# A token loop of the first mixture-of-experts layer, moved from ahead of the last down product to between the sixth and the seventh expert tile

## The chip, the cores and the metric

One core of one Trainium2 chip. The metric is the time of one execution of the whole kernel in device microseconds. The kernel before has a median of 1263.22 us.

## The reference

Two layers over 256 tokens and 256 context tokens of width 1024. Each layer has a mixer (differential attention, latent attention and retention side by side), a layer norm, a grouped mixture of 16 experts with two experts to a token, and a second layer norm. The first layer (l = 0) routes all 512 rows through its experts, the second only the 256 tokens. The change is inside the first layer's mixture:

```python
def moe(tokens, router_w, router_b, w1, w3, w2):
    scores = jax.nn.sigmoid((tokens @ router_w).astype(jnp.float32))
    choice = scores + router_b.astype(jnp.float32)
    ...
    gates = jnp.sum(jax.nn.one_hot(eidx, N_EXPERTS, ...) * wsel[..., None], 1)

    def expert_step(acc, p):
        w1e, w3e, w2e, ge = p
        y = (jax.nn.silu(tokens @ w1e) * (tokens @ w3e)) @ w2e
        return acc + ge[:, None] * y, None
    out, _ = lax.scan(expert_step, jnp.zeros_like(tokens), (w1, w3, w2, gates.T))
    return out
```

w1 and w3 are 1024 x 512 and w2 is 512 x 1024 for each expert, all in 32-bit floats.

## The kernel before, in words

**Expert tiles.** The mixture of the first layer is cut into twelve tiles of 128 token places (`PLANS[0]`, NX = 12). A tile of one expert has all its places for that expert; a tile of two shares them between two. In order of work the tiles are: one, one, two, one, one, two, one, two, one, two, one, one. Step t of the loop over tiles writes `up(t)` (the products with w1 and w3, L1625 for one expert, L1653 for two), then `tokens(t + 1)` (the next tile's rows are turned, L2003), then `down(t - 1)` (the product with w2, L1625 or L1750). `hidden` (L1668) turns the gated hidden rows; `combine` (L2033, L2036) brings a tile's result back to token order; `ones_at` and `transposed_ones` (L1617) make the 0/1 matrices for that; `lists` make the next index list (L1601) and gather rows by it (L1982). TensorE's order is the order in which this is written (`manual_schedule(engines=only_pe)`); the other engines' order is planned by the scheduler.

**Weights.** For a tile of one expert each weight piece of 128 x 2048 (1 MB) is split in two halves of 128 x 1024: `wsplit` casts the high part on ACT (`wh`), and DVE (640 columns) and POOL (384 columns, L1231) make the low part (`wl`); then three products are made from high and low parts. A tile of two experts uses its weights as they came. A `Stream` loads the pieces in order into a ring of ten buffers: SP issues a load (L184 as two halves of 512 KB, L188 as one of 1 MB) as soon as a buffer comes free, so that the order of loads is fixed and buffers set their pace. Up to eight of SP's loads are under way at a time.

**Rows by token.** Down products of tiles 0 to 6 (`BY_ROWS` = 7) are written as rows to a buffer in memory: ACT issues `yd<-rows` (L1688), two of 256 KB for a tile. `token_rows` (L1972) gathers them for each token at step t = 9, on POOL, in eight gathers.

**The loop.** A tile has a fixed number of places. For tokens that found none there is a loop, `with tc.For_i(0, beyond, 1)`, whose number of passes is a register with the count of such extra tiles. Its body gathers tokens, loads one expert's weights, makes the products and adds them to the stream `xT`. In the kernel before it stands at L2095, behind `hidden(11)`, two of the combines, and two weight pieces that are split ahead (`wsplits`), and ahead of the last down product (`down(NX - 1, ..., pieces=pieces)`, L1708). The second layer has a loop of its own (L1883).

The lines around the loop:

```python
                for c in range(2):
                    pieces += wsplits()
            for _ in range(2):
                ws.drop_ring()
            with tc.For_i(0, beyond, 1):
                ei, pj, gj = next_beyond()
                ...
                    add_to_stream(k, oc)
            ws.rings[0]["limit"] = 10 ** 9
            ...
                down(NX - 1, more + [[]], pieces=pieces)
```

Of the kernel before, what the change touches and what calls it, by code (L numbers as in the profile page):

```python
# [9 lines left out]
F32 = mybir.dt.float32  # L10
F32R = mybir.dt.float32r
# [3 lines left out]
ALU = mybir.AluOpType  # L15
# [211 lines left out]
def build(tc, x_in, ctx_in, wada, win, wout, wexp, wqkv, rw, prm_in, bro_in, lnr, cst_in, out, dbg=None):  # L227
# [170 lines left out]
    def level():  # L398
        load["A"] = load["V"] = 0.0
# [789 lines left out]
    for l in range(DEPTH):  # L1189
# [395 lines left out]
        def ones_at(t):  # L1585

            Os[t] = []
            for i in tiles:
                O = rp_.tile([128, 128], F32, tag="O", name="O", bufs=2 * NT)
                for n, s in enumerate(slots_of(l, t)):  # L1590
                    pos = (pos0 if s < 2 else posm)[:, i, s:s + 1]
                    if n == 0:
                        V.tensor_scalar(O, C("iota"), pos, None, op0=ALU.is_equal)
                    else:
                        V.scalar_tensor_tensor(O, C("iota"), pos, O, op0=ALU.is_equal, op1=ALU.add)
                Os[t].append(O)
# [32 lines left out]
        def up(t, between):  # L1629

            o = sbig()
            x = xs_of.pop(t)
            for c in range(4):
                if len(plan[t]) == 1:
                    xH, xL = x
                    if not first_splits:
                        raw = ws.take()
                    ob = o[:, halves[c // 2]]
                    early = len(first_splits) > 0
                    for q in range(2):  # L1640
                        h, lo = first_splits.pop(0) if early else wsplit(raw[:, 1024 * q:1024 * q + 1024])
                        kk = 4 * (c % 2) + 2 * q
                        mm6([(ob, xH[:, kk + k, :], xL[:, kk + k, :], h[:, halves[k]], lo[:, halves[k]]) for k in range(2)],
                            kk == 0, kk == 6, (0, 2, 1))
                    if not early:
                        ws.done()
                else:
                    for c2 in range(2):
                        raw = ws.take()
                        for q in range(2):  # L1650
                            kk = 4 * (c % 2) + 2 * c2 + q
                            for r0, r1, e in groups(t):
                                T.matmul(o[r0:r1, halves[c // 2]], lhsT=x[:, kk, r0:r1], rhs=raw[e][:, halves[q]],  # L1653
                                         start=(kk == 0), stop=(kk == 7), skip_group_check=True)
                        ws.done()
                for s in between[c]:
                    s()
            u = ex.tile([128, 512], F32, tag="u", name="u", bufs=2)
            A.activation(u, o[:, 0:512], AF.Sigmoid)
            V.scalar_tensor_tensor(u, u, gms.pop(t), o[:, 0:512], op0=ALU.mult, op1=ALU.mult)  # L1660
            V.tensor_mul(u, u, o[:, 512:1024])
            us[t] = u

        def hidden(t):
            u = us[t]
            tp = tpb()
            for k in range(4):
                T.transpose(tp[:, 128 * k:128 * k + 128], u[:, 128 * k:128 * k + 128], ident)  # L1668
            uH = ex.tile([128, 4, 128], F32R, tag="uH", name="uH", bufs=2)
            d = uH.rearrange("p k t -> p (k t)")  # L1670
            if len(plan[t]) == 1:
                uL = ex.tile([128, 4, 128], F32R, tag="uL", name="uL", bufs=2)
                A.copy(d, tp)
                V.tensor_sub(uL.rearrange("p k t -> p (k t)"), tp, d.bitcast(F32))
                us[t] = uH, uL
            else:
                copy(d.bitcast(F32), tp)
                us[t] = uH[:].bitcast(F32)
# [104 lines left out]
        if last:  # L1783
# [49 lines left out]
            def combines(j):  # L1833
                return [lambda n=n: combine(j, n, lambda i: f[:, i]) for n in range(2)]
# [97 lines left out]
        else:  # L1932
# [35 lines left out]
            def token_rows():  # L1968

                for n, op in enumerate((ALU.bypass, ALU.add)):  # L1970
                    for i in tiles:
                        g = G.indirect_dma_start(out=by_token_[i], out_offset=None, in_=yd[:, :],  # L1972
                                                 in_offset=bass.IndirectOffsetOnAxis(ap=twoi[:, i, n:n + 1], axis=0),
                                                 bounds_check=ZROW, oob_is_err=False, compute_op=op)
                return g.ins
# [66 lines left out]
            def combines(t, rows=None):  # L2042
                return [[lambda k=k: combine(t, k, rows=rows) for k in (2 * q, 2 * q + 1)] for q in range(4)]

            level()
            with tc.manual_schedule(engines=only_pe):
                for t in range(2):
                    ones_at(t)
                    lists(t)
                ws.pump(after=gms[1])  # L2050
                for t in range(2):
                    to_tokens(t)
                tokens(0)
                at_slots()
                ones_at(2)
                for t in range(NX):
                    steps = [[] for _ in range(4)]
                    if t > BY_ROWS + 1:
                        steps = combines(t - 2, by_token_ if t == BY_ROWS + 3 else None)
                    if t:  # L2060
                        steps[0].insert(0, lambda t=t: hidden(t - 1))
                    if t + NXG < NX:
                        ones_at(t + NXG)
                    if t == BY_ROWS + 2:

                        with tc.issue_after(last_split[0]):
                            last_rows = token_rows()
                    up(t, steps)
                    if t + 1 < NX:
                        tokens(t + 1)  # L2070
                    if t == 0:
                        lists(2)
                        to_tokens(2)
                    if t == 1:
                        beyond = tiles_beyond()
                        rows_of_tokens()
                    more = [[], [lambda t=t: lists(t + NXG)], [], [lambda t=t: to_tokens(t + NXG)]]
                    if t + NXG >= NX:
                        more = [[]] * 4
                    if t:  # L2080
                        with tc.issue_after(last_rows) if t == BY_ROWS + 2 else nullcontext():
                            down(t - 1, more)
                    else:
                        for x in sum(more, []):
                            x()
                hidden(NX - 1)
                pieces = []
                more = combines(NX - 2)
                for x in more.pop(0):
                    x()  # L2090
                for c in range(2):
                    pieces += wsplits()
            for _ in range(2):
                ws.drop_ring()
            with tc.For_i(0, beyond, 1):  # L2095
                ei, pj, gj = next_beyond()
                O = [rp_.tile([128, 128], F32, tag="O", name="O", bufs=2 * NT) for _ in tiles]
                for i in tiles:
                    V.tensor_scalar(O[i], C("iota"), pj[:, i:i + 1], None, op0=ALU.is_equal)
                ll = acc()  # L2100
                sums_at(ll[:, 0:2], O, lambda i: gj[:, i])
                xb = ring2.tile([128, 2048], F32, tag="w", name="xb", bufs=RB[l][1])
                xb, ot = xb[:, 0:1024], xb[:, 1024:1024 + W]
                G.memset(xb, 0.0)
                gather(xb, ll)
                gpl = small("gpl", [1])
                V.tensor_copy(gpl, ll[:, 0:1])
                transposed_ones(ot, O)
                xo = ex.tile([128, 8, 128], F32R, tag="xH", name="xo")[:].bitcast(F32)
                place(xo, xb)  # L2110
                yy = sbig()
                beyond_products((xo[:, 0:4], xo[:, 4:8]), ei, yy, from_ring)
                yo = ex.tile([128, 8, 128], F32R, tag="xL", name="yo")[:].bitcast(F32)
                V.tensor_scalar_mul(yo, yy.rearrange("p (k c) -> p k c", c=128), gpl)
                for k in range(8):
                    oc = acc()
                    T.matmul(oc, lhsT=yo[:, k], rhs=ot, start=True, stop=True)
                    add_to_stream(k, oc)
            ws.rings[0]["limit"] = 10 ** 9
            ws.known = marks["known", 1]  # L2120
            ws.pump()
# [165 lines left out]
```

## Time and profile before

| | |
|---|---|
| time, median of 3 runs | 1263.22 us (1261.75 to 1264.92) |
| profiled execution, own time | 1265.02 us |
| its span | 1263.1 us |
| PE busy | 1147.8 us, 91% |
| DVE, ACT, POOL busy | 666.5, 475.9, 350.1 us |
| moved by DMA | 310.72 MB, mean 246 GB/s |

All times of the profile are counted from the start of the span. The granted TensorE clock is given as a share of full speed: 1.00 is 2.4 GHz and 0.50 is 1.2 GHz. "DMA share" is the mean busy share of the core's 16 DMA engines; it can be a little over 1 where packets overlap. A number in brackets at the end of a timeline row is the time for which the engine stood idle ahead of it, and what ended that. The first layer's expert tiles take the stretch from 406 to about 722 us; the new place of the loop is at 541 us, the old one at 704 us.

### The profile page before, as it was taken

The numbers are of one execution on the slowest core, as the hardware profiler recorded it, in microseconds if no ns is written. First come the engines' busy times: TensorE is split into PE (matmuls) and PEld (weight loads), VectorE is DVE, ScalarE is ACT, GpSimd is POOL, SyncE is SP. The second block draws the span as 40 slices with busy tenths as digits, with TensorE's granted clock in tenths as the row PEclk, the third lists the DMA queues.
The fourth block names the chain that finished last, engine by engine and source line by source line (L and its number), as shares of the span: only waits on it lengthen the run. The fifth ranks groups of instructions, "written<-read, shape, count | busy, mean of one in ns | idle before, by whom it ended". The sixth has DMA issues, their size and how long they took to land. (4 is left out here: it accounts for less than half of the span.)

```text
span 1263.1 us, 18014 instructions
## 1 busy us (share of the span) xinstructions
PE 1147.8 (91%) x6483; PEld 755.9 (60%) x6483; DVE 666.5 (53%) x1340; ACT 475.9 (38%) x878; POOL 350.1 (28%) x344
## 2 busy tenths in 40 slices
PE   6999999998996798998979689999988699999994
PEld 4898764556785655555456578975556544444431
DVE  3545376626568857654477767537546812222116
ACT  4423456335235444433244364545443210111102
POOL 0242210222033544543464356221131100101002
PEclk9999999998996899999989889999998799999997
DMA  9533008771445889999996202411665899999981
GB/s 349 179 141 132 1 1 300 268 266 67 172 162 228 311 325 383 404 406 414 400 351 249 75 31 102 171 34 61 239 267 187 322 410 407 409 408 409 409 327 60
DMA packets 72301, 310.72 MB, mean 246 GB/s; under 512 B 8576, under 2 KB 9744, under 8 KB 57872
## 3 DMA queue, kind: packets, MB, share of 16 engines
q1 hardware_dynamic: 63952, 287.73, 59.2%
q10 hardware_dynamic: 5376, 13.40, 2.9%
q0 software_dynamic: 2880, 8.39, 2.2%
q8 instruction: 53, 0.87, 0.3%
q14 instruction: 40, 0.33, 0.1%
HBM read 304.70 MB, written 6.89 MB: 247 GB/s over the span
## 5 line engine op out<-in xcount | busy, mean ns | idle before, releaser
L222 DVE TENSOR_TENSOR wl<-w,wh 128x640 fp32r<-128x640 f32 (+3 forms) x133 | 163.3, 1247 | 54.5 <-ACT wh L222 53.1
L222 ACT CAST wh<-w 128x1024 fp32r<-128x1024 f32 (+2 forms) x135 | 132.7, 1006 | 104.0 <-PE s L433 34.7
L1231 POOL TENSOR_TENSOR wl<-w,wh 128x384 fp32r<-128x384 f32 x96 | 131.3, 1405 | 109.3 <-ACT wh L222 107.0
L1653 PE MATMUL s<-w,x 128*64 128x512 f32 (+1 forms) x640 | 115.8, 596 | 0.0
L222 DVE TENSOR_REDUCE mxv<-s 128x2 f32<-128x1024 f32 (+1 forms) x54 | 56.3, 1043 | 47.8 <-PE s L1099 18.6
L222 ACT ACTIVATE P<-s,mxv 128x512 f32<-128x512 f32 (+1 forms) x108 | 65.9, 618 | 39.1 <-DVE mxv L222 22.3
L1750 PE MATMUL s<-w,uH 128*32 128x512 f32 (+1 forms) x480 | 78.5, 595 | 0.0
L1653 PEld LDWEIGHTS s<-w,x 128*64 128x64 f32 (+1 forms) x640 | 33.6, 126 | 64.9 <-issue 61.4
L222 ACT ACTIVATE u<-s 128x512 f32<-128x512 f32 x20 | 11.9, 596 | 122.5 <-PE s L1653 114.2
L222 DVE TENSOR_TENSOR yL<-s,yH 128x512 fp32r<-128x512 f32 x24 | 16.5, 687 | 78.5 <-ACT yH L222 78.4
L431 PE MATMUL acc<-wh,hH 128*128 128x384 f32 (+3 forms) x148 | 52.8, 360 | 4.8 <-ACT hH L222 4.8
L432 PE MATMUL s<-wl,hH 128*128 128x384 f32 (+2 forms) x148 | 52.9, 358 | 2.9 <-DVE wl L222 2.9
L1653 PE MATMUL s<-w,xH 128*32 128x512 f32 (+1 forms) x352 | 53.6, 595 | 0.0
L431 PE MATMUL s<-wh,hH 128*128 128x384 f32 (+2 forms) x148 | 52.9, 357 | 0.0
L433 PE MATMUL s<-wh,hL 128*128 128x384 f32 (+2 forms) x148 | 52.7, 356 | 0.0
L432 PE MATMUL acc<-wl,hH 128*128 128x384 f32 (+3 forms) x148 | 52.2, 353 | 0.0
L433 PE MATMUL acc<-wh,hL 128*128 128x384 f32 (+3 forms) x148 | 50.7, 352 | 0.0
L1750 PEld LDWEIGHTS s<-w,uH 128*32 128x32 f32 (+1 forms) x480 | 23.2, 122 | 45.0 <-issue 43.2
L1625 PE MATMUL s<-wl,xH 128*128 128x512 f32 x128 | 43.4, 415 | 7.0 <-DVE wl L222 6.4
L222 DVE SCALAR_TENSOR_TENSOR u<-u,gp,s 128x512 f32<-128x512 f32 x20 | 14.8, 742 | 64.9 <-ACT u L222 64.9
L500 PE MATMUL acc<-w,sc 128*32 128x512 f32 x320 | 45.7, 602 | 1.7 <-DMA w<-in_wada_dram 1.6
L1797 POOL TENSOR_TENSOR xr<-xr,lr 128x1024 f32<-128x1024 f32 x4 | 9.4, 2360 | 135.0 <-ACT lr L222 135.0
(530 smaller groups left out, 2546.8 us busy)
## 6 DMA issues: line engine op xcount, KB each, us to landing
w<-in_wexp_dram SPq DMA_DIRECT2D x284, 512.0 KB, 10.2
w<-in_wexp_dram SPq DMA_DIRECT2D x48, 1024.0 KB, 9.9
w<-in_wada_dram SPq DMA_DIRECT2D x46, 1024.0 KB, 6.9
w<-in_win_dram SPq DMA_DIRECT2D x8, 1024.0 KB, 4.9
w<-in_wout_dram SPq DMA_DIRECT2D x8, 1024.0 KB, 7.8
w<-in_win_dram SPq DMA_DIRECT2D x9, 768.0 KB, 4.9
row<-rowd ACTq DMA_DIRECT2D x9, 512.0 KB, 7.7
yd<-rows ACTq DMA_DIRECT2D x14, 256.0 KB, 6.7
```

Source lines behind the costliest of these rows:

```text
L222: return f(*args, **kw)
L431: T.matmul(o, lhsT=lh, rhs=rh, start=start, stop=False, skip_group_check=True)
L432: T.matmul(o, lhsT=lh, rhs=rl, start=False, stop=False, skip_group_check=True)
L433: T.matmul(o, lhsT=ll, rhs=rh, start=False, stop=stop, skip_group_check=True)
L500: T.matmul(box["o"][32 * c:32 * c + 32, :], lhsT=sc32[:, k, :], rhs=w[:, 512 * c:512 * c + 512], start=(k == 0), stop=(k == 7), skip_group ...
L1231: last_split[0] = G.tensor_tensor(lo[:, c:], raw[:, c:], h[:, c:].bitcast(F32), op=ALU.subtract).ins
L1625: T.matmul(o, lhsT=ll if ps_ == 2 else lh, rhs=rl if ps_ == 1 else rh, start=start and j == 0 and not (same and n), stop=stop and j == 2 a ...
L1653: T.matmul(o[r0:r1, halves[c // 2]], lhsT=x[:, kk, r0:r1], rhs=raw[e][:, halves[q]], start=(kk == 0), stop=(kk == 7), skip_group_check=True)
L1750: T.matmul(o[r0:r1, halves[n]], lhsT=u[:, kk, r0:r1], rhs=raw[e][:, halves[n]], start=(kk == 0), stop=(kk == 3), skip_group_check=True)
L1797: G.tensor_tensor(x1[:, i, :], x1[:, i, :], lr, op=op)
```

## The change

The loop is taken from behind the twelve tiles and written as a function, `tokens_beyond`, that is called between step t = 5 and step t = 6: behind up(5), tokens(6) and down(4), and ahead of up(6). The body's steps are the same. Its buffers are others: `fr[0]` and `fr[1]`, which so far hold two early weight pieces and from step 9 the gathered token rows, and `wh`/`wl` buffers for its weights, in place of ring buffers and the tiles' own. Lines behind it move, for example L2095 becomes L2047.

```diff
+            def tokens_beyond(beyond):
+
+                with tc.For_i(0, beyond, 1):
+                    ei, pj, gj = next_beyond()
+                    xb, ot = fr[0][:, 0:1024], fr[0][:, 1024:1024 + W]
+                    O = [fr[0][:, 1536 + 128 * i:1664 + 128 * i] for i in tiles]
+                    xo, yo = (fr[1][:, 1024 * n:1024 * n + 1024].rearrange("p (k c) -> p k c", c=128) for n in range(2))
...
+                    beyond_products((xo[:, 0:4], xo[:, 4:8]), ei, yy,
+                                    lambda: [hlp.tile([128, 1024], F32R, tag=x, name="wo")[:].bitcast(F32) for x in ("wh", "wl")])
...
+                        add_to_stream(k, oc)
...
-                for t in range(NX):
-                    steps = [[] for _ in range(4)]
...
+            for t0, t1 in ((0, 6), (6, NX)):
+                if t0:
+                    tokens_beyond(beyond)
+                with tc.manual_schedule(engines=only_pe):
+                    for t in range(t0, t1):
+                        steps = [[] for _ in range(4)]
...
+            with tc.manual_schedule(engines=only_pe):
                 hidden(NX - 1)
...
             for _ in range(2):
                 ws.drop_ring()
-            with tc.For_i(0, beyond, 1):
-                ei, pj, gj = next_beyond()
-                O = [rp_.tile([128, 128], F32, tag="O", name="O", bufs=2 * NT) for _ in tiles]
...
-                xb = ring2.tile([128, 2048], F32, tag="w", name="xb", bufs=RB[l][1])
...
-                beyond_products((xo[:, 0:4], xo[:, 4:8]), ei, yy, from_ring)
...
-                    add_to_stream(k, oc)
             ws.rings[0]["limit"] = 10 ** 9
```

TensorE at the old place, in the kernel before: the first five rows are the end of the loop's body, L2095 the loop itself, L1708 the last down product. Ahead of the body stand the loop's entry and four products L2036, combines of tile 10.

```order
L2003 MATMUL tp<-cst,xb 128x128 x8
L1555 MATMUL s<-wo,xo 128x512 x16
L1563 MATMUL tp<-cst,uo 128x128 x4
L1569 MATMUL s<-wo,xo 128x512 x8
L2117 MATMUL acc<-xb,yo 128x512 x8
L2095 REGISTER_ALU
L2095 COMPARE_AND_BRANCH
L2095 UNCONDITIONAL_BRANCH
L1708 MATMUL s<-wh,uH 128x512
L1708 MATMUL s<-wl,uH 128x512
L1708 MATMUL s<-wh,uL 128x512
```

TensorE at the same place in the changed kernel:

```order
L1668 MATMUL tp<-cst,u 128x128 x4
L2036 MATMUL acc<-OT,yH 128x512
L2036 MATMUL acc<-OT,yL 128x512
L2036 MATMUL acc<-OT,yH 128x512
L2036 MATMUL acc<-OT,yL 128x512
L1708 MATMUL s<-wh,uH 128x512
L1708 MATMUL s<-wl,uH 128x512
L1708 MATMUL s<-wh,uL 128x512
```

The loop is gone from between the combines and the last down product, and nothing else moved there.

ACT at the new place, in the kernel before: w_4541 is the last piece of the tile before, w_4573 and w_4583 are the first pieces for the seventh tile and the next ones, `yd<-rows` are the two row writes of down(4).

```order
L222 CAST wh<-w_4541 128x1024 x2
L222 CAST wh<-w_4573 128x1024 x2
L222 CAST OT<-tp 128x512
L1688 DMA yd<-rows 128x512
L222 COPY rows<-s 128x512
L222 CAST wh<-w_4583 128x1024 x2
L1688 DMA yd<-rows 128x512
```

The same in the changed kernel, where these pieces are named w_4544, w_4576 and w_4586, L2047 is the loop, and the rows of `fr` and `uo` are its body; ahead of the first row stand the casts of w_4544, the cast of OT and the first row write:

```order
L222 COPY rows<-s 128x512
L1501 TENSOR_LOAD nxi
L2047 COMPARE_AND_BRANCH
L2047 UNCONDITIONAL_BRANCH x2
L2290 BRANCH_PREFETCH_HINT
L222 COPY fr_3490<-tp 128x512
L222 COPY fr_3491<-tp 128x512 x2
L222 ACTIVATE uo<-s 128x512
L2047 REGISTER_ALU
L2047 COMPARE_AND_BRANCH
L2047 UNCONDITIONAL_BRANCH
L1688 DMA yd<-rows 128x512
```

The second row write stands behind the loop now, and behind it the casts of w_4576 and w_4586: the seventh tile's first piece, which was cast ahead of OT before, is cast behind the loop.

SP at the new place in the changed kernel: w_4742 is the last weight piece that is issued ahead of the loop, and the next follows behind it.

```order
L184 DMA w_4742<-in_wexp_dram 128x1024
L184 ISA
L184 DMA w_4742<-in_wexp_dram 128x1024
L1501 TENSOR_LOAD nxi
L2047 COMPARE_AND_BRANCH
```

In the kernel before, that piece (named w_4739 there) and the next are issued one behind the other:

```order
L184 DMA w_4739<-in_wexp_dram 128x1024
L184 ISA
L184 DMA w_4739<-in_wexp_dram 128x1024
L184 ISA
L184 DMA w_4790<-in_wexp_dram 128x1024
```

So a load that followed at once now has the loop ahead of it.

## Rows read from the trace of the kernel before

**Rows 1.** The page: busy time, share and instructions of PE, and DVE's splits.

```profile
PE 1147.8 (91%) x6483; PEld 755.9 (60%) x6483; DVE 666.5 (53%) x1340; ACT 475.9 (38%) x878; POOL 350.1 (28%) x344
L222 DVE TENSOR_TENSOR wl<-w,wh 128x640 fp32r<-128x640 f32 (+3 forms) x133 | 163.3, 1247 | 54.5 <-ACT wh L222 53.1
```

**Rows 2.** Windows: length, busy PE, PEld, DVE, ACT, POOL, PEclk, DMA share, GB/s.

```profile
557.00:612.00 55.00, 51.08 (x272) 27.36 (x270) 26.02 (x37) 17.81 (x24) 19.16 (x14) 0.97 1.02 412
...
650.00:672.00 22.00, 21.53 (x113) 17.68 (x112) 16.31 (x25) 12.65 (x15) 16.63 (x11) 0.99 1.02 401
672.00:704.00 32.00, 30.35 (x140) 20.82 (x138) 27.65 (x43) 17.22 (x21) 15.13 (x13) 1.00 0.39 148
sum 147.00, PE 133.97 PEld 80.67 DVE 89.77 ACT 56.37 POOL 67.69; mean PE 26.79 PEld 16.13 DVE 17.95 ACT 11.27 POOL 13.54
```

**Rows 3.** Waits of PE, 545 to 704: us in total, times, longest.

```profile
PE s L1625 <- DVE wl L222: 6.7, 2, 5.7
PE s L1625 <- ACT wh L222: 2.6, 2, 1.7
...
PE tp L2003 <- DVE OT L222: 1.3, 1, 1.3
```

**Rows 4.** Line L188, SP's load that is issued at 616.4.

```profile
DMA to landing us min/median/max: 14.8/14.8/14.8
```

**Rows 5.** Timeline of ACT: start, us, operation [idle before, what ended it].

```profile
637.22 2.00 ACT L222 CAST wh<-w 128x1024 fp32r<-128x1024 f32 x2
...
665.55 1.05 ACT L222 CAST wh<-w 128x1024 fp32r<-128x1024 f32 x1 [4.51 <-DMA w<-in_wexp_dram]
```

**Rows 6.** Timeline of PE at the old place.

```profile
710.46 0.79 PE L1708 MATMUL s<-wh,uH 128*128 128x512 f32 x1 [6.25 <-SPq L2095]
...
711.48 0.63 PE L1708 MATMUL s<-wh,uL 128*128 128x512 f32 x1
```

**Rows 7.** Windows, shorter stretches.

```profile
544.00:548.00 4.00, 4.00 (x13) 3.22 (x14) 2.92 (x3) 1.88 (x2) 2.99 (x2) 0.57 1.04 411
645.00:650.00 5.00, 5.00 (x12) 3.88 (x13) 3.33 (x5) 1.58 (x2) 1.65 (x1) 0.50 1.05 279
708.00:709.00 1.00, 0.00 (x0) 0.00 (x0) 0.00 (x0) 0.00 (x0) 0.00 (x0) 0.50 0.03 12
710.40:715.20 4.80, 4.74 (x11) 3.77 (x12) 0.92 (x3) 0.00 (x0) 0.00 (x0) 0.50 0.01 2
715.20:722.00 6.80, 6.80 (x30) 5.28 (x29) 5.30 (x12) 3.61 (x6) 2.85 (x2) 1.00 0.00 0
```

**Rows 8.** Line L2095, the loop, on ACT: durations in ns, first and last start.

```profile
L2095 ACTq COMPARE_BRANCH  x3: 38/38/58, 704.3 to 709.9; - x3
```

**Rows 9.** Timeline of DVE at the old place.

```profile
704.84 0.68 DVE L222 TENSOR_TENSOR uL<-tp,uH 128x512 fp32r<-128x512 f32 x1
```

**Rows 10.** Waits of PE, 722 to 1000, the longest.

```profile
PE acc L1420 <- DVE seb L222: 6.0, 1, 6.0
```

**Rows 11.** Timeline of PE at the new place.

```profile
540.49 0.60 PE L1617 MATMUL tp<-cst,O 128*128 128x128 f32 x4
...
543.98 0.80 PE L1625 MATMUL s<-wl,xH 128*128 128x512 f32 x2 [1.97 <-DVE wl L222]
```

**Rows 12.** Line L184, SP's last load ahead of the new place.

```profile
L184 SPq DMA_DIRECT2D w<-in_wexp_dram x1: 333/333/333, 541.7 to 541.7; - x1
...
DMA to landing us min/median/max: 11.5/11.5/11.5
```

**Rows 13.** Timeline of ACT at the new place.

```profile
543.88 1.05 ACT L222 CAST wh<-w 128x1024 fp32r<-128x1024 f32 x1
544.31 0.33 ACTq L1688 DMA_DIRECT2D yd<-rows  x1
```

**Rows 14.** Timeline of POOL, first and last of eight gathers of token rows.

```profile
614.76 0.99 POOL L1972 DMA_INDIRECT fr<-yd,twoi  x1 [0.30 <-issue]
...
638.57 1.56 POOL L1972 DMA_INDIRECT fr<-yd,twoi  x1 [2.07 <-DMA fr<-yd,twoi]
```

**Rows 15.** Timeline of PE behind those gathers.

```profile
644.75 1.22 PE L1625 MATMUL s<-wl,uH 128*128 128x512 f32 x2 [5.67 <-DVE wl L222]
```

More of the change, by code (lines that the diff above doesn't have):

```diff
@@ L2043, in combines @@
                 return [[lambda k=k: combine(t, k, rows=rows) for k in (2 * q, 2 * q + 1)] for q in range(4)]
+            def tokens_beyond(beyond):
[4 more added lines that the diff above has]
+                    xo, yo = (fr[1][:, 1024 * n:1024 * n + 1024].rearrange("p (k c) -> p k c", c=128) for n in range(2))
+                    for i in tiles:
+                        V.tensor_scalar(O[i], C("iota"), pj[:, i:i + 1], None, op0=ALU.is_equal)
+                    ll = acc()
+                    sums_at(ll[:, 0:2], O, lambda i: gj[:, i])
+                    G.memset(xb, 0.0)
+                    gather(xb, ll)
+                    gpl = small("gpl", [1])
+                    V.tensor_copy(gpl, ll[:, 0:1])
+                    transposed_ones(ot, O)
+                    place(xo, xb)
+                    yy = sbig()
+                    beyond_products((xo[:, 0:4], xo[:, 4:8]), ei, yy,
+                                    lambda: [hlp.tile([128, 1024], F32R, tag=x, name="wo")[:].bitcast(F32) for x in ("wh", "wl")])
+                    V.tensor_scalar_mul(yo, yy.rearrange("p (k c) -> p k c", c=128), gpl)
+                    for k in range(8):
+                        oc = acc()
+                        T.matmul(oc, lhsT=yo[:, k], rhs=ot, start=True, stop=True)
+                        add_to_stream(k, oc)
             level()
@@ L2055, in build @@
                 ones_at(2)
-                for t in range(NX):
-                    steps = [[] for _ in range(4)]
[L2058 to L2085, printed above, removed]
@@ new lines, in build @@
+            for t0, t1 in ((0, 6), (6, NX)):
[4 more added lines that the diff above has]
+                        steps = [[] for _ in range(4)]
+                        if t > BY_ROWS + 1:
+                            steps = combines(t - 2, by_token_ if t == BY_ROWS + 3 else None)
+                        if t:
+                            steps[0].insert(0, lambda t=t: hidden(t - 1))
+                        if t + NXG < NX:
+                            ones_at(t + NXG)
+                        if t == BY_ROWS + 2:
+                            with tc.issue_after(last_split[0]):
+                                last_rows = token_rows()
+                        up(t, steps)
+                        if t + 1 < NX:
+                            tokens(t + 1)
+                        if t == 0:
+                            lists(2)
+                            to_tokens(2)
+                        if t == 1:
+                            beyond = tiles_beyond()
+                            rows_of_tokens()
+                        more = [[], [lambda t=t: lists(t + NXG)], [], [lambda t=t: to_tokens(t + NXG)]]
+                        if t + NXG >= NX:
+                            more = [[]] * 4
+                        if t:
+                            with tc.issue_after(last_rows) if t == BY_ROWS + 2 else nullcontext():
+                                down(t - 1, more)
+                        else:
+                            for x in sum(more, []):
+                                x()
@@ L2094, in build @@
                 ws.drop_ring()
-            with tc.For_i(0, beyond, 1):
-                ei, pj, gj = next_beyond()
-                O = [rp_.tile([128, 128], F32, tag="O", name="O", bufs=2 * NT) for _ in tiles]
[L2098 to L2101, printed above, removed]
-                xb = ring2.tile([128, 2048], F32, tag="w", name="xb", bufs=RB[l][1])
[L2103 to L2111, printed above, removed]
-                beyond_products((xo[:, 0:4], xo[:, 4:8]), ei, yy, from_ring)
[L2113 to L2117, printed above, removed]
-                    add_to_stream(k, oc)
             ws.rings[0]["limit"] = 10 ** 9
```

## Prediction

> **What bounds the kernel now.** I read the page first: TensorE (PE) is busy for 91% of the span [rows 1], so a change that moves one wait is priced by what it does to PE at two places, not by any engine's total. Then the windows over the tiles behind the new place: from 557 to 704 PE is busy for 134.0 of 147.0 us, while the DMA engines carry a share of 1.02 in most of it [rows 2]. Both look full, so I read whom PE waits for: in 545 to 704 above all for splits that DVE and ACT make, 6.7 and 2.6 us, and never for a load [rows 3]. The loads run ahead: one issued at 616.4 lands 14.8 us later, at 631, and the next casts of weights start at 637.2 [rows 4, 5]. One cast does wait 4.5 us for its load, at 665, but PE is busy for 21.5 of the 22.0 us around it [rows 5, 2]. So behind the new place PE sets the pace, and what it loses at 541 it carries to 704.
>
> The loop makes no pass in this run: its body's last product (L2117) has no record. What it costs is being entered and left, and the trace shows that at the old place. The first product behind the loop starts at 710.46, after 6.25 us idle that are put down to SP's L2095 [rows 6]; the one ahead ended at 704.2. The DMA moves almost nothing any more in 708 to 709 (share 0.03), ACT leaves the loop at 709.9 [rows 7, 8]. I read this as: all wait until SP has seen its last load land, and are then let out within 1 to 2 us.
>
> **What the change removes.** PE goes from 704.2 straight into the last down product. Its first two products need only uH; the third needs uL, which DVE ends at 704.84 + 0.68 = 705.52 [rows 9]. So the third starts at about 705.55 and not at 711.48 [rows 6]: 5.9 us. Behind the old gap PE ran at half clock (0.50, 1.2 GHz) until 715.2: 11 products in 4.8 us, 0.43 apart, and then 30 in 6.8, 0.23 apart [rows 7]. From 711.48 to 715.2 that is 3.7 us at half speed, 1.9 lost. What stays of the gap is about 1 us, and such waits between 672 and 704 left the clock at 1.00 [rows 2], so I take the 1.9 in full; but a gap of 1.97 us at 543.98 did lower it, so the bound is none of it. Sum **-7.8** (bound -5.9). Behind 722 PE waits for DVE and ACT only, at longest 6.0 us [rows 10], and their work there starts from PE's results, so the gain is kept.
>
> **What it adds.** In the new place PE enters behind four transposes, at 540.49 + 0.60 = 541.1 [rows 11]. SP enters behind a load that it issues at 541.7 and that lands 11.5 us later, at 553.2, since the queue is full [rows 12]. A row write by ACT (256 KB, issued at 544.31) now stands behind the loop, which takes 0.6 us at 411 GB/s out of the queue: 552.6. At the old place ACT left 0.9 us or more behind the last bytes, so I let it out 0.8 us after the landing (bounds 0.5 and 2): 553.4. It then issues that row write (0.33) and casts the first half of the next tile's first weight (1.05) [rows 13], which it had done well ahead of PE and now does inside the gap: PE restarts at about 555.0. Its first four products, at half clock 0.43 apart, take until 556.7, when the low half (DVE 1.25 behind the cast [rows 1]) is just there. Before, that fifth product started at 543.98, after 1.97 us idle [rows 11]: 12.7 us later. Before, too, the clock fell to half behind that small gap: 0.57 over 544 to 548 [rows 7] is 3.5 us at half, 1.7 lost. Now it stays half for 4.8 us as at the old place, of which 3.1 lie past 556.7, 1.6 lost: -0.1. Sum **+12.6**. Bounds: 10.5, if SP's loads land earlier and ACT is out at 552; 15, if the release takes 2 us and the splits come one by one to a PE that is ahead of them.
>
> DVE, POOL and SP are held too. DVE's and POOL's splits of that weight are those PE now waits for, and are counted. SP's next load waits until that weight is split, about 557, so the DMA moves nothing for 6 to 7 us. I cost this at nothing: at 553 all ten buffers are full, and at 2.6 us for 1 MB (410 GB/s) they last PE for over 20 us; PE, 12.6 late, leaves the loads more room than before. Without this cover it is rival one.
>
> Sum 12.6 - 7.8 = **+4.8 us**. The profiled execution took 1265.02 us, 1.9 more than its span and 1.8 above the median 1263.22; a difference inside its span I put on the median: 1263.2 + 4.8 = **1268.0 us**. About 0.3% (3.8 us: 1259.4 to 1267.0) is what a measurement of this kernel can tell from no change, so the forecast lies just past it.
>
> **Rival one: the loads set the pace.** Then PE's lateness at 555 is made up in its waits behind that, and only the time in which the DMA moved nothing counts: 6 to 8 us added, 7.8 less, about **1262.5**. For it: the share of 1.02, and the cast that waited 4.5 us at 665 [rows 2, 5]. Against it: no wait of PE for a load, and loads that land 6 us and more ahead [rows 3 to 5]. In 557 to 612 PE's matrix products fill 51.1 of 55.0 us, its weight loads only 27.4 [rows 2]. The Trainium skill (Perfetto Trace Analysis, Identifying the Most-Contended Engine) judges TensorE's headroom by the share of its weight loads, not of busy products, and names the engine of highest occupancy as the one that counts; by that rule the DMA is the bound here, and the time this rival's. The products' spacing of 0.23 us at full clock, with nothing between them, speaks for PE all the same. Chance 0.18.
>
> **Rival two, faster: the lateness is swallowed.** The second half of the tiles has a hole of its own: POOL's eight gathers of token rows stand from 614.76 to 640.1, waiting for the DMA, and only then does POOL split weights, so PE stands 5.67 us until 644.75 and runs at half clock (0.50) to 650 [rows 14, 15, 7]. If the gathers don't move with PE, or go faster as fewer bytes wait ahead of them, PE arrives 12 us later at splits that are ready: 5.67, 2.6 of the 5.3 us at half clock, and the 1.3 us wait for OT just ahead [rows 3] come back. The change then adds 3.0 and takes 7.8: about **1258.4**. The point from which it decides: whether the first gather starts near 615 or near 627. Against it: the gather ahead of it takes an index from PE's list product, so the chain starts from PE. Chance 0.10.
>
> **Rival three: worse.** After the drain three engines split weights with nothing ready, and the first two tiles stutter: another 3 to 6 us with the clock at half for longer, **1272**. For it: nearly all of PE's waits are for splits [rows 3]. Against: they are short in the stretch from 557 to 612 (clock 0.97 [rows 2]). Chance 0.15. That the loop doesn't move as the text says, or that an exit costs nothing that can be seen, so that the time stays: 0.02.
>
> **How the numbers follow.** Forecast 0.55, with its own range 1264.5 to 1271, two thirds of it past 1267.0. Slower by over 0.3%: 0.37 + 0.15 = 0.52. Same: 0.18 of the forecast, 0.15 of rival one, 0.02 of rival two, 0.02 of the last. Faster: 0.03 of rival one and 0.08 of rival two. The range 1260 to 1274 leaves out most of rival two, the lower end of rival one and the top of rival three.
>
> **What would show it.** In the changed profile: a PE gap of 13 to 14 us from 541, put down to SP's loop line; a DMA share near 0 for some 6 us up to 559; the clock at 0.5 for about 5 us; no gap over 2 us ahead of the last down product; the gathers at about 627, and the hole behind them as large as before; still no wait of PE for a load. I am wrong if the gap at 541 is under 9 us, if the hole at 640 shrinks, or if PE waits for loads.

## The result, and the profile after

The changed kernel takes **1270.87 us** (median of 8 runs, 1267.43 to 1273.84) against 1263.07 us of the kernel before (8 runs beside it): a ratio of 1.0062, 95% interval 1.0046 to 1.0078, or 5.8 to 9.9 us slower. Forecast were 1268.0 us, slower, in a range of 1260 to 1274.

At the new place, the timeline of PE in the changed kernel (start, us, operation, and in brackets the idle time ahead and what ended it):

```profile
541.27 0.60 PE L1617 MATMUL tp<-cst,O 128*128 128x128 f32 x4
555.47 1.22 PE L1625 MATMUL s<-wh,xH 128*128 128x512 f32 x2 [13.60 <-ACT wh L222]
...
557.35 1.05 PE L1625 MATMUL s<-wl,xH 128*128 128x512 f32 x2
...
560.87 0.71 PE L1625 MATMUL s<-wh,xH 128*128 128x512 f32 x2
```

PE stands for 13.6 us. It reached the place 0.78 us later than in the trace of before (541.27 for 540.49 [rows 11]); the product that started at 543.98 there starts at 557.35 here, so the place costs it 12.6 us up to that point. Who holds it is seen on SP's last load ahead of the loop, which is issued at 542.3, on ACT and on the loop's line:

```profile
DMA to landing us min/median/max: 10.9/10.9/10.9
```

```profile
554.01 0.33 ACTq L1688 DMA_DIRECT2D yd<-rows  x1
554.38 4.83 ACT L222 CAST wh<-w 128x1024 fp32r<-128x1024 f32 x5 [9.80 <-SPq L2047]
```

```profile
L2047 SPq EVENT_SEMAPHORE  x21: 17/27/28, 543.2 to 554.9; - x21
...
L2047 ACTq COMPARE_BRANCH  x3: 38/38/58, 545.1 to 553.9; - x3
```

The load lands at 553.2. ACT had been waiting since 544.6; it leaves the loop at 553.9, writes its rows and casts, and the first cast releases PE. Meanwhile the queue runs dry, as the windows show (busy PE, PEld, DVE, ACT, POOL; PEclk; DMA share; GB/s):

```profile
541.00:553.00 12.00, 0.87 (x6) 0.50 (x5) 1.47 (x5) 1.17 (x2) 0.29 (x1) 0.73 0.93 369
553.00:556.00 3.00, 0.53 (x1) 0.50 (x2) 0.55 (x1) 1.62 (x2) 0.49 (x1) 0.50 0.27 96
556.00:560.00 4.00, 4.00 (x11) 3.06 (x10) 3.88 (x4) 3.21 (x4) 4.00 (x3) 0.50 0.03 10
560.00:566.00 6.00, 6.00 (x30) 4.95 (x29) 6.00 (x5) 3.65 (x4) 6.00 (x5) 0.98 0.98 315
```

Against a share of 1.02 the DMA engines lose 1.1 + 2.3 + 4.0 + 0.2 = 7.6 us of work. The clock is at 1.2 GHz (0.50) from 553 to 560 and near full speed (0.98) from 560 to 566.

At the old place the 6.25 us [rows 6] have shrunk to this:

```profile
716.28 0.39 PE L1708 MATMUL s<-wh,uH 128*128 128x512 f32 x1
716.51 0.40 PE L1708 MATMUL s<-wl,uH 128*128 128x512 f32 x1
717.80 0.80 PE L1708 MATMUL s<-wh,uL 128*128 128x512 f32 x1 [0.89 <-DVE uL L222]
718.39 0.63 PE L1708 MATMUL s<-wh,uH 128*128 128x512 f32 x1
```

```profile
718.00:720.00 2.00, 2.00 (x5) 1.63 (x6) 1.12 (x3) 0.00 (x0) 0.00 (x0) 0.50 0.80 323
720.00:722.00 2.00, 2.00 (x9) 1.56 (x9) 1.23 (x4) 0.00 (x0) 0.00 (x0) 0.84 0.01 3
```

The third product waits for uL only, but the clock falls here all the same. The gathers of token rows moved with PE, from 614.76 [rows 14] to 627.48, and the hole behind them stayed, 4.1 us with 1.6 us just ahead of it for 5.67 [rows 15]:

```profile
627.48 0.99 POOL L1972 DMA_INDIRECT fr<-yd,twoi  x1 [0.30 <-issue]
```

```profile
651.88 0.82 PE L1625 MATMUL s<-wh,uH 128*128 128x512 f32 x2 [1.62 <-ACT wh L222]
656.80 1.22 PE L1625 MATMUL s<-wl,uH 128*128 128x512 f32 x2 [4.10 <-DVE wl L222]
```

### The profile page after: what moved, and what is told of

It is laid out like the page before. It is cut to its first block, busy times and chain, and to the rows that moved or that the text cites. A ratio compares the mean times of both kernels' runs of the same rounds, so it can differ in the third digit from the quotient of the medians.

```text
span 1269.4 us, 18024 instructions
## 1 busy us (share of the span) xinstructions
PE 1146.9 (90%) x6483; PEld 754.6 (59%) x6483; DVE 664.9 (52%) x1334; ACT 479.5 (38%) x884; POOL 354.1 (28%) x344
## 5 line engine op out<-in xcount | busy, mean ns | idle before, releaser
L222 ACT ACTIVATE u<-s 128x512 f32<-128x512 f32 x20 | 11.9, 595 | 123.9 <-PE s L1653 114.2
L1625 PE MATMUL s<-wh,xH 128*128 128x512 f32 x128 | 43.3, 421 | 14.6 <-ACT wh L222 14.6
```

Of the source, the lines that this page charges most:

```text
L222: return f(*args, **kw)
L1625: T.matmul(o, lhsT=ll if ps_ == 2 else lh, rhs=rl if ps_ == 1 else rh, start=start and j == 0 and not (same and n), stop=stop and j == 2 a ...
```

## The experiments

For every run the table has PE's lateness against the trace of before: the start of the same product (the n-th with the same operands) in both traces, less what it was at 534 us, ahead of the new place. Columns: behind the new place (574), ahead of the old one (675), behind it (736), in times of the trace of before; then the medians against the runs of before beside them.

| run | 574 | 675 | 736 | median, us | against before, us | ratio, 95% interval |
|---|---|---|---|---|---|---|
| changed kernel | 11.9 | 11.5 | 5.1 | 1270.87 | +7.8 | 1.0046 to 1.0078 |
| no loop | -0.3 | -1.7 | -8.6 | 1256.76 | -6.5 | 0.9935 to 0.9969 |
| four loads held | 4.3 | 8.6 | 3.3 | 1266.09 | +2.9 | 1.0008 to 1.0041 |
| body without split buffers | 10.4 | 12.2 | 5.9 | 1269.18 | +5.9 | 1.0031 to 1.0068 |
| splits ahead | 16.1 | 17.6 | 11.5 | 1274.36 | +11.1 | 1.0065 to 1.0111 |
| low part last | 11.4 | 12.1 | 4.3 | 1270.32 | +7.3 | 1.0044 to 1.0078 |
| old place, loads held | 0.0 | -0.7 | -3.9 | 1259.64 | -3.4 | 0.9956 to 0.9986 |
| held, rows by POOL | 2.9 | 9.9 | 1.7 | 1266.21 | +3.1 | 1.0007 to 1.0036 |
| before, 4 MB more | 3.9 | 8.1 | 6.7 | 1272.95 | +9.3 | 1.0056 to 1.0106 |
| before, 2 MB more | 3.8 | 3.2 | 3.1 | 1268.97 | +5.3 | 1.0025 to 1.0060 |
| changed, 2 MB more | 12.1 | 13.4 | 5.6 | 1270.33 | +6.7 | 1.0042 to 1.0081 |

A single execution strays by 1 to 2 us, at times more, in places that no edit touches, so the medians decide and the columns say where.

**The two places, one by one.** The loop is taken out altogether, and with it the work for tokens that found no place, of which this data has none:

```diff
-                if t0:
-                    tokens_beyond(beyond)
```

> Edit: the changed kernel without the first layer's loop in either place (tokens beyond the tiles, of which this data has none, are left out). My theory (TensorE sets the pace, a loop costs what TensorE stands for it): against the kernel before only the old place's cost goes, 5.9 us of waiting, with the clock still falling for a moment as in the changed kernel: about 6 us less than before, 1257; the changed kernel is then 13 to 14 us above it: 11.9 us measured at the new place, the rest from places not yet named. Rival, the loads set the pace: less than 4 us faster than before, since the old place's loads were idle anyway and the expert tiles end when their loads do. Rival, the move also costs something away from the two places: the difference between the changed kernel and this one is over 14 us.

Measured: 1256.76 us. The old place was worth 6.5 us (3.9 to 8.2 by the interval), and the new one costs 1270.87 - 1256.76 = 14.1 us. The changed kernel's own trace has 11.9 us at the new place; with an error of nearly 3 us on the 14.1, the runs don't tell whether a little is lost elsewhere too. The clock fell at the old place without any loop there, behind the 1.42 us wait for yL: products at full speed take 0.39 us in these rows, at half 0.63.

```profile
701.61 0.50 PE L2036 MATMUL acc<-OT,yL 128*128 128x512 f32 x1 [1.42 <-DVE yL L222]
...
702.48 0.63 PE L1708 MATMUL s<-wh,uH 128*128 128x512 f32 x1
702.91 0.63 PE L1708 MATMUL s<-wl,uH 128*128 128x512 f32 x1
703.93 0.80 PE L1708 MATMUL s<-wh,uL 128*128 128x512 f32 x1 [0.39 <-DVE uL L222]
```

**Is the gap SP's drain? Fewer loads ahead of it.**

```diff
                     for t in range(t0, t1):
+                        if t == 3:
+                            ws.known = 103
...
                     tokens_beyond(beyond)
+                    mark = small("mark", [128])
+                    held = S.dma_start(mark[0:1], xT[0:1, 1, 7, 0:128])
+                    with tc.issue_after(held.ins):
+                        ws.known = marks[l]
+                        ws.pump()
```

> Edit: the changed kernel with the last four weight pieces (4 MB) ahead of the loop issued behind it; a small copy by SP behind the loop keeps them there. My theory (the gap is SP's drain of the queue, and PE carries the gap to the end): the last landing comes some 10 us sooner, the other engines arrive at about 545, PE restarts near 548 instead of 555.5, gap 6 to 7 us instead of 13.6; about 7 us less than the changed kernel, 1264. Rival, the loads set the pace: the DMA stands for as long as before, so the time stays at 1270 to 1271 and PE waits for loads behind the loop. Rival, the gap is the price of the loop itself (semaphores, branches): the gap stays over 10 us.

Measured: the gap is what the theory gave, the time only half of it: 4.8 us less than the changed kernel. PE stands 5.66 us at the new place and then 6.01 us at 606, on a cast (PE's timeline, then ACT's):

```profile
546.37 1.22 PE L1625 MATMUL s<-wh,xH 128*128 128x512 f32 x2 [5.66 <-ACT wh L222]
...
606.69 1.22 PE L1625 MATMUL s<-wh,xH 128*128 128x512 f32 x2 [6.01 <-ACT wh L222]
```

```profile
602.25 3.22 ACTq L1688 DMA_DIRECT2D yd<-rows  x2
605.59 1.99 ACT L222 CAST wh<-w 128x1024 fp32r<-128x1024 f32 x2 [6.94 <-DMA w<-in_wexp_dram]
```

So the gap is the drain, and behind it something else sets the end, with SP's loads in it.

**More loads ahead of the gap, with the splits ready.** First the body's weights go into the rooms `fr`, which lets the scheduler put the seventh tile's splits ahead of the loop:

```diff
-                                    lambda: [hlp.tile([128, 1024], F32R, tag=x, name="wo")[:].bitcast(F32) for x in ("wh", "wl")])
+                                    lambda: (xb, fr[1][:, 1024:2048]))
```

> Edit: the changed kernel with the loop body's weight halves in the rooms fr instead of the split buffers wh and wl, so that the seventh tile's first splits stand ahead of the loop. My theory: the same drain, but PE restarts as the loop lets it out, about 1.3 to 1.8 us sooner (no cast behind the loop), gap near 12 us: 1269. Rival three of the prediction (the restart stutters because nothing is split): more, 4 us and over, 1266 or less. Rival, the loads set the pace: SP's next load is issued 2 to 3 us sooner, so also about 1268 to 1269; this run does not tell those two apart.

Then two pieces' splits are also written there, so that SP has two more buffers to fill before it enters:

```diff
                 if t0:
+                    for _ in range(2):
+                        first_splits += wsplits()
                     tokens_beyond(beyond)
```

> Edit: as the run before, with the splits of two pieces written ahead of the loop, so that SP issues two more loads (2 MB) ahead of it. My theory: the drain grows by 2 times 2.6 us, PE's gap to about 17 us, and the time by about 5 us against the run before, 1274, although the DMA now stands less. Rival, the loads set the pace: the DMA stands 2 us or less, so faster than the run before by 3 us or more, 1265. The two forecasts lie 9 us apart.

Measured: 1269.18 and 1274.36, both as the theory had it. PE's gap in the first and in the second:

```profile
552.18 1.22 PE L1625 MATMUL s<-wh,xH 128*128 128x512 f32 x2 [12.70 <-SPq L2047]
```

```profile
557.22 1.22 PE L1625 MATMUL s<-wh,xH 128*128 128x512 f32 x2 [18.26 <-SPq L2047]
```

2 MB more in the queue make the gap 5.6 us longer and the kernel 5.2 us slower, although SP had brought the DMA further. That nothing is split at the restart cost the 1.7 us between the changed kernel and the first of these, which is within the error of some 3 us.

**What gave the gain back.** A completion counter tells when a transfer has landed. The row writes `yd` on ACT and SP's loads take eight such counters in turn, and each waits until the transfer ahead of it on its counter has landed. Of the program with the loads held, the row writes of tile 6 and what they wait for:

```
L1688 DMA yd<-rows 128x512 [waits DMAHW1_49,Activation_49]
L1688 DMA yd<-rows 128x512 [waits DMAHW3_49,Activation_49]
```

The transfers ahead of them on DMAHW1 and DMAHW3 are halves of two weight loads, which SP issued at 587.16 and 592.12; ACT issues the two writes at 602.25 and 605.15, 15.1 and 13.0 us later. So tile 6's writes are given to POOL:

```diff
-                    nc.scalar.dma_start(yd[128 * t:128 * t + 128, halves[n]], rows)
+                    (nc.gpsimd if t == 6 else nc.scalar).dma_start(yd[128 * t:128 * t + 128, halves[n]], rows)
```

> Edit: the run with four loads held, and the two row writes (yd) of tile 6 issued by POOL instead of ACT. With the loads held PE lost 5.5 us again at 600: ACT stood until 605.5 at these two row writes, with the next tile's casts queued behind them. Theory (the row writes share their completion counters with SP's loads and wait for loads that are still under way, so ACT's queue hands the loads' lateness on to PE): the wait of 6.0 us at 606 goes, 4 to 5 us less than with the loads held, 1261 to 1262. Rival (the next tile's weights themselves had not landed; the loads set the pace): the wait stays, now for the load, and the time stays at 1266.

Measured: the wait at 606 is gone, the time is the same, 1266.21. In the profiled execution (1263.39 us, the second fastest of 12) the loss moved on to 670 (ACT, DVE and PE there):

```profile
669.62 1.99 ACT L222 CAST wh<-w 128x1024 fp32r<-128x1024 f32 x2 [9.89 <-DMA w<-in_wexp_dram]
```

```profile
670.70 2.36 DVE L222 TENSOR_TENSOR wl<-w,wh 128x640 fp32r<-128x640 f32 x2 [6.55 <-ACT wh L222]
```

```profile
673.99 1.09 PE L2033 MATMUL acc<-cst,fr 128*128 128x128 f32 x4 [5.26 <-DVE xr L222]
```

It is the cast that waited 4.51 us for its load in the kernel before [rows 5]; now it waits 9.89, DVE's split stands behind it, and PE behind DVE's xr, which is queued behind that split. PE is 2.7 us late at 660 and 9.4 at 672. The cast starts 7.6 us late against the trace of before. That is about what the DMA engines lost around the loop: shares of 0.71, 0.49, 0.20 and 0.85 in the four stretches of 4 us from 533 to 549, or 7.3 us of work against a share of 1.02. The counters were a way in which late loads reach PE, not the only one. That the loads themselves are a bound was then tried without any loop.

**Loads alone, nothing held.** The kernel before, with loads that nobody reads behind the last load ahead of the new place (8 or 4 of 512 KB):

```diff
+                    if t == 6:
+                        with tc.issue_after(ws.load_of[106]):
+                            for x in range(8):
+                                c = slice(1024 * (x // 2 % 2), 1024 * (x // 2 % 2) + 1024)
+                                S.dma_start(fr[x % 2][:, c], wexp[l, x, 0, :, 0:1024])
                     up(t, steps)
```

> Edit: the kernel before with 4 MB of loads that nobody reads (into the rooms fr, idle then): 2 MB behind the last load ahead of the new place, 2 MB a few loads later; 10.3 us of the queue at 410 GB/s, and no loop at the new place. In the runs with the loads held PE's gap shrank by 8 us and most of it was given back at 600 or at 670, where casts waited for loads. Theory now (two bounds lie side by side: PE can be 12 us late at 541, or the loads 8 us late, for nearly the same end; the loads have 2 us or less to spare): the whole 10 us or most of them reach the end, 1271 to 1274. The prediction's own reading (loads land 6 us and more ahead, PE sets the pace): at most 4 us, 1263 to 1267.

> Edit: the kernel before with the first 2 MB of these loads alone, 5.1 us of the queue. Theory of two bounds: 3 to 5 us more than before, 1266 to 1268. The prediction's reading: no change, 1263.

Measured: 9.3 us more (7.1 to 13.4) for 10.3 us of the queue, and 5.3 more (3.2 to 7.6) for 5.1, near what the theory of two bounds gave. The traces show another way for it. PE's waits in the run with 4 MB (us in total, times, longest), between 545 and 720, and ACT's:

```profile
PE s L1625 <- ACT wh L222: 10.1, 3, 6.2
```

```profile
ACT rows L222 <- DMA w<-in_wexp_dram: 12.9, 2, 7.0
ACT wh L222 <- DMA w<-in_wexp_dram: 7.7, 3, 5.2
```

In the kernel before casts wait 5.0 us for loads in that stretch, and row copies not at all. The row copies stand behind row writes. In the run with 2 MB ACT's and PE's timelines read:

```profile
546.21 0.33 ACTq L1688 DMA_DIRECT2D yd<-rows  x1
546.57 0.59 ACT L222 COPY rows<-s 128x512 f32<-128x512 f32 x1 [6.71 <-DMA w<-in_wexp_dram]
```

```profile
548.15 0.74 PE L1625 MATMUL s<-wh,xH 128*128 128x512 f32 x2 [1.87 <-ACT wh L222]
```

In the kernel before this row write was issued at 543.03. With 4 MB it goes at 548.97; of the weight load issued at 538.5, the one ahead of it on its counter, the trace says:

```profile
  ACT rows L222: 7.0, 1
DMA to landing us min/median/max: 10.4/10.4/10.4
```

538.5 and 10.4 is 548.9. In the kernel before the row write has another counter, whose load had been issued at 531.5: the four loads that nobody reads took four counters and so moved the row write on to a later load. PE is 3.8 us late by this, at 556 in the times of the trace of before, and, with 2 MB, 3.2 at 675; with 4 MB the second row write of this kind, at 606, adds 6 us. The cast at the load that was tight before waits as long as it did then, 4.53 us for 4.51 [rows 5]. So these two runs don't show that the weight loads had nothing to spare. That rests on the run with POOL's row writes, where a cast did wait for its own load.

And the changed kernel with the same 2 MB, behind the first load that follows the loop:

> Edit: the changed kernel with the same 2 MB behind the first load that follows the loop. The DMA stood 8.1 us there, so the loads are then 13.2 us late, and PE 12 to 13. Theory of two bounds (the later of the two counts, not their sum): 0 to 3 us more than the changed kernel, 1271 to 1274. Rival, the two add up: 5 us more, 1276. The prediction's reading: no change, 1271.

Measured: 1270.33, the changed kernel's own time within the error; 5.1 us more of the queue cost nothing once PE was 12 us late anyway, while in the kernel before they cost 5.3. This is what the later of the two latenesses gives, and also what the prediction's reading gave; that they add up is excluded. (This run's profiled execution, 1275.65 us, lost 5 us more around 760 to 790; the median has nothing of it.)

**The clock at the old place.**

```diff
-                        h, lo = pieces[kk]
-                        for j, (lh, r) in enumerate(((uH, h), (uH, lo), (uL, h))):
...
+                        if kk % 2 == 0:
+                            todo = [(u_, k, x) for u_ in (uH, uL) for k in (kk, kk + 1) for x in pieces[k][:1 + (u_ is uH)]]
+                        for _ in range(3):
+                            lh, k, x = todo.pop(0)
```

> Edit: the changed kernel with the last down product's order turned within each pair of weight pieces: the four products that need only uH first, the two with uL behind them. In the changed kernel PE waits 0.89 us for uL at the old place, and the clock is at half for 2.7 us behind that, which is why the clock's 1.9 us did not come back there. My theory: the wait goes and the clock stays at full speed, 2 us less than the changed kernel, 1269. Rival: the clock falls behind the 1.41 us wait for yL that stands ahead, so only 0.9 us comes back, 1270.

Measured: 1270.32, 0.5 us less with an error of about 2 us: this doesn't decide between the two. In its one profile the clock did stay up (1.00 in 715 to 717), with 0.44 us of waiting left:

```profile
716.29 0.73 PE L1710 MATMUL s<-wh,uL 128*128 128x512 f32 x2 [0.44 <-DVE uL L222]
```

**A version that beats both.** The drain at the old place can be taken away where it hurts nobody: nobody uses the loads of `win`, weights of the next stage, that are issued ahead of the loop until the first cast of them, at 718.2 in the kernel before.

```diff
             ws.known = marks["known", 1]
-            ws.pump()
+            mark = small("mark", [128])
+            held = S.dma_start(mark[0:1], xT[0:1, 1, 7, 0:128])
+            with tc.issue_after(held.ins):
+                ws.pump()
```

> Edit: the kernel before, loop at the old place, with the three win loads that SP had issued ahead of the loop issued behind it (held by a small copy by SP). My theory (the old gap of 6.25 us, too, is SP's drain): the gap ends when the last engine arrives, DVE at 707.0, and the release of 0.7 us behind it: PE restarts near 708 instead of 710.5, about 2.5 us less than the kernel before, 1260.5; the loads land by 718, ahead of the split at 724. Rival: the win loads come too late and a cast waits for them behind 722, so no gain or slower, 1263 to 1266.

Measured: 1259.64, faster than the kernel before by 3.4 us (ratio 0.9971, 0.9956 to 0.9986). The gap is 3.19 us and ends with DVE, no longer with SP, and no cast waits for a load behind it, though the first of them is at 713.7 (the expectation had 724):

```profile
705.82 0.80 PE L1708 MATMUL s<-wh,uH 128*128 128x512 f32 x1 [3.19 <-DVEq L2095]
```

## Why the prediction was right, step by step

**Direction and size.** Slower was forecast, by 4.8 us, and slower it is, by 7.8 (5.8 to 9.9). The sum was 12.6 - 7.8; against the kernel without a loop the terms come out as 14.1 and 6.5, with errors of nearly 3 and of 2 us. Both forecasts lean towards the change, so they don't make up for each other.

**The new place, +12.6: right.** SP's drain, the release, the row write and the cast were each where the prediction put them: 13.6 us of gap for 13.9, the fifth product 12.6 us late for 12.7. The runs with less and with more in the queue show that the drain is the cause: the gap goes from 13.6 to 5.7 us with 4 MB less, and from 12.7 to 18.3 with 2 MB more.

**"I take the 1.9 in full": the term that failed.** Of -7.8 at the old place the 5.9 for the third product came (11.5 to 5.1 in the table is 6.4 in all), but of the clock's 1.9 no more than 0.5: with the loop gone, waits of 1.41 and 0.89 us stayed, and the clock fell behind them. The bound of -5.9 that the prediction kept was the right value. It had argued from a wait between 672 and 704 that left the clock at 1.00; in the run with no loop it fell behind that very wait.

**"I cost this at nothing: at 553 all ten buffers are full": the number held, the reason didn't.** The DMA's 7.6 us cost nothing here, but not because the loads run ahead: in the run with POOL's row writes, where PE came out of the loop only 2.9 us late, 7.3 us of DMA work lost made PE 9.9 us late at 675. They cost nothing since PE was later still. "Loads that land 6 us and more ahead" was read off single loads; the same page of rows had the cast at 665 that waited for its load [rows 5], and in that run that one had no slack left for the engines behind it.

**Rival one** was wrong as a time (1262.5), and right as a bound: had PE been less than some 8 us late at 541 (an estimate from the 7.3 and 7.6 us of DMA work lost), the loads would have set the end, as they do at 670 in the run with the loads held and POOL's row writes. The Trainium skill (Perfetto Trace Analysis, Identifying the Most-Contended Engine) says to optimise first the engine of highest occupancy, and takes HBM utilization for the DMA in its place. This case's traces agree in so far as DMA work lost reached PE once PE was not later itself (7.3 us lost, 9.9 us late); that the DMA alone bounds the kernel before no run here shows.

**Rival two** fell: the gathers moved by 12.7 us with PE, and the hole came with them. **Rival three**, 3 to 6 us for a restart that stutters, found no support: with the casts ahead of the loop PE is 1.5 us less late at 574 (10.4 for 11.9), and the medians differ by 1.7 with an error of some 3.

**What stays open.** The traces show 5.1 us between the two places, the medians 7.8 with an error of 2. A stray of 1 to 2 us of the one execution of before, which lost 1.7 us more between 534 and 675 than the run without a loop does in the same code, covers most of that; it wasn't tried any further.

## What to carry to other kernels

A loop whose number of passes is a register cost time here even with no passes (a gap of 13.6 us at the new place, 6.25 at the old one): all engines waited until the loads that were under way had landed. So look at what the queue holds where it stands, and hold loads back that nobody needs soon (that alone gave 3.4 us at the old place). Where two engines both look full, try the slack instead of arguing it: put in a few loads that nobody reads, and then look in the trace where the time goes, since here the added loads cost PE its first 3.8 us over the counters of the row writes and not over late weights. And of two latenesses that run side by side the later one counts, so shortening the longer one pays only down to the other: 8 us off the gap brought 4.8, and taking the row writes' wait out as well brought no more.

## What the runs showed of the hardware

ACT's own small writes waited for SP's big loads: in the run with four loads held a row write of 256 KB stood until 605.1 us for a load's completion counter, and the casts behind it on ACT with it; in the run with 4 MB more another was issued 0.1 us behind the landing of such a load. Four loads put in ahead of it moved it to another counter and made PE 3.8 us late. The clock behind the same 1.4 us wait for yL was not the same in each kernel: at 1.2 GHz for 2.7 us in the changed kernel (with 0.89 us more of waiting), fallen in the run without a loop already ahead of the next wait (of 0.39), at 2.4 GHz throughout in the run with the low part last (0.44 more).
